# Hybrid retention/HGRN2 step on one core: fewer full warm-up matmuls, row scales of x1 through DRAM, W_v work in the ramp, and a new placement table

## The chip, the cores and the metric

The kernel runs on one core of one Trainium2 chip. The metric is the device time of one launch in microseconds. Each launch is timed as a whole; a profiled launch gives the span from the first to the last instruction and what every engine did in it: PE (TensorE matmul), PEld (TensorE weight load), DVE (VectorE), ACT (ScalarE), POOL (GpSimd) and SP (SyncE, which here only issues DMAs).

## The reference

One layer of a decoder: 2048 prompt tokens and 8 single new tokens, width 1024. The normalised input is projected to eight groups of 512 columns (q, k, v and gate of retention; q, forget, input and gate of HGRN2), two chunked recurrences with 4 heads each run over the tokens, their outputs are normalised and gated, joined, projected, added to the input and normalised again.

```python
h = rmsnorm(x, norm_g)
p = (h @ w_in).astype(jnp.float32)
rq, rk, rv, rg, hq, hf, hi, hgate = jnp.split(p, 8, axis=-1)
...
o_ret, s_ret_new = chunked_decay_recurrence(rq, rk, rv, log_gamma, s_ret)   # rq, rk rotated
o_ret = head_rmsnorm(o_ret, ret_g) * jax.nn.silu(rg)
...
o_hg, s_hg_new = chunked_decay_recurrence(silu(hq), kin, hi, logf, s_hg)
o_hg = head_rmsnorm(o_hg, hg_g) * jax.nn.silu(hgate)
y = x + jnp.concatenate([o_ret, o_hg], axis=-1) @ w_out
return rmsnorm(y, final_norm_g), ...      # and the four new states
```

All data are fp32.

## The kernel before

**Products.** The matrix products run in a form with seven instead of eight block products (sums such as S1, S2, T1, T2 of blocks are made first). Every fp32 operand X is split in two fp32r parts, a high part `Xh` and a low part `Xl`, and a product is three matmuls for each pair of blocks (high·high, low·high, high·low). One block product is 12 matmuls of 128x512. Seven of them make a *unit*. Units u = -6 to -1 compute the values (V) of both recurrences, u = 0 to 23 the gates (G), the q and k of HGRN2 (H) and of retention (R) of one head and one half of the tokens each, u = 24 to 31 the output projection (O). Names such as aG, bG, eH are the PSUM banks that the products of a unit fill; x0… and x1… are the blocks of the first and of the second half of the tokens, wo… those of the output weights; r24S, w24S are a unit's raw and split weight blocks.

**The ramp.** Before unit -6 stands a prologue written out in order: loads of the first token block (`tok_load0`, tile x0r) and of the W_v weights (`wv_load`, tile wvr), their splits (`x_split0`, `wv_split`), and plain products `pv` of the first half row (lines 465 to 650) while the sums and differences of the W_v blocks (`wv_subs`, `wv_parts`: the T1 to T4 and their splits) are made. 13 matmuls of 128x128 and 17 of 32x8 on a tile of ones (`wu`, lines 200 and 203) go ahead of the first product. Each of these fp32 matmuls stands in the profile as two records.

**The queue of events.** Everything that is not a block product is put between the products by `at(pos, f)`: `f` is issued when the products have come to position `pos`, counted in products (7 to a unit, fractions inside a product). The positions stand in one table, `AT`, written by hand; for unit u most are `7 * u + AT[...]`. The engines' queues are in order, so the table sets what stands ahead of what on PE, DVE, ACT, POOL and SP:

```python
SLOTS = (
    (0, "A11", "B11", "A", True), (1, "S1", "T1", "E", True), (3, "S2", "T2", "A", False),
    (4, "S4", "B22", "E", False), (5, "A12", "B21", "B", True), (6, "S3", "T3", "A", False),
    (9, "A22", "T4", "A", False),
)
```

gives the seven products with their place, their weight-side and token-side operand and their bank.

**The parts that the change touches.** `hgrn_rec` and `ret_rec` are the recurrence of one head: scores (`plh`, `pah`, 32x16 and 32x64 matmuls, lines 1223 to 1284, which read the tiles qth and kh that DVE has scaled, lines 1188 and 1191), state updates, outputs and norms; their steps are placed by `AT['hgrn']` and `AT['ret']`. `swap_events` replaces the token blocks x0… by x1… (positions `AT['swap']`, base 77) and then by the output weights wo… (`AT['swapo']`, base 161): a DMA of 1 MB (line 1465), a split on ACT (line 709) and one on DVE (line 713). `blocks_sums` makes the token-block sums of V units with `less` (line 434), whose 16 subtractions of 128x512 stand partly on DVE, partly on POOL. The tokens' row scales `rs_all` hold one token on each partition; to scale x1 blocks along their free axis, `x1_dg` puts them on diagonals (DVE), `x1_spread` multiplies by ones (PE, tile prb, line 701), copies (ACT, line 702) and stores 256 KB to `rb_dram` (POOL, line 1327), which `x1_rb` loads again (line 1345). The same is done in small for the new tokens (`decode_dg`, `decode_spread`, tile prsd). The last half row of the output (`i == 7`) ends with an add to the residual (tile xro, line 716), a square sum (line 1639), a power on POOL (line 1650), the scaling and two stores.

Of the kernel before, what the change touches and what calls it, by code (L numbers as in the profile page):

```python
# [24 lines left out]
NB = 8  # L25
# [23 lines left out]
def spooled(u):  # L49
# [10 lines left out]
          'load': 18.0,  # L60
# [10 lines left out]
 'ret': {'load': 12.0,  # L71
# [4 lines left out]
         'o0': 15.5,  # L76
         'st1': 15.7,
         'o1': 17.1,
         'last': 17.6,
         't0': 19.01,  # L80
         't1': 21.7},
# [6 lines left out]
       'sS1': -1.4,  # L88
# [3 lines left out]
       'sA12': 1.4,  # L92
       'sS3': 2.4,
       'sA22': 3.05},
 're': {'A11': -3.4, 'S1': -2.4, 'S2': -1.4, 'S4': -0.4, 'A12': 0.6, 'S3': 1.6, 'A22': 2.6},
 'dec': {'mm': -1.97, 'mm0': -3.42, 'copy': -0.9, 'copy0': -2.4, 'sel': 0.7},
# [6 lines left out]
          'lT4': 12.2,  # L103
          'B11': (3.0, 3.0, 3.5, 3.5),
          'T1': (6.5, 6.5, 7.0, 7.0),
          'T2': (8.2, 8.2, 8.7, 8.7),
          'B22': (8.9, 8.95, 9.2, 9.75),
          'B21': (9.45, 9.85, 10.0, 10.3),
          'T3': (11.3, 11.3, 11.8, 11.8),
          'T4': (14.2, 14.2, 14.7, 14.7)},  # L110
# [11 lines left out]
           'B21': (9.45, 9.85, 10.0, 10.3),  # L122
           'T3': (11.3, 11.55, 11.8, 12.05),
           'T4': (14.2, 14.2, 14.7, 14.7)},
 'x1': (21.0, 41.0, 48.0, 63.0),
 'x1s': (0.5, 1.8, 1.9, 3.4, 5.0),
 'wo': (27.0, 69.0, 101.8, 122.8),
 'wos': (0.0, 2.3, 3.3),
 'wu': 17,
 'wop': (140.0, 1.8, 2.0, 2.6),  # L130
 'gate': {'G': 0.7, 'store': 1.2, 'R': 0.8, 'H': 0.7, 'root': 0.5, 'scale': 1.0, 'gt': 1.2, 'tr': 0.6},
 'fin': 0.75,
# [11 lines left out]
 'dhs': (-5.0, -2.2, -2.2, -1.5)}  # L144
# [5 lines left out]
def step_kernel(ctx, tc, a, out):  # L150
# [22 lines left out]
    vd_dram = dr.tile([2, NB, GW], F32, tag="vd_dram", name="vd_dram")  # L173
    v_dram = [
# [24 lines left out]
    for n in range(13):  # L199
        pe.matmul(wu, ones, ones, start=True, stop=True)  # L200
# [146 lines left out]

    spread_to = {}

# [74 lines left out]
    def blocks_sums(i, n):  # L424
# [8 lines left out]
        def less(o, x, y):  # L433
            (dve if (i, n) in ((6, 0), (7, 1)) else pool).tensor_tensor(o, x, y, op=ALU.subtract)
# [35 lines left out]
    def tok_load0(i, k0, cuts=1):  # L470
        r = x0r[i, k0] = t_get([P, 2, 256], f"x0r{i}{k0}")
        for n in range(0, 2, 2 // cuts):
            kk = slice(n, n + 2 // cuts)
            sp.dma_start(r[:, kk], a["x_t"][V_ORDER[i], :, k0 + kk.start : k0 + kk.stop])
# [101 lines left out]
    dgd = vq.tile([NB, NB], F32, tag="dgd", name="dgd")  # L576

    def decode_dg():
        dve.tensor_scalar(dgd, ident[:NB, :NB], rsd[:, 1:2], None, op0=ALU.mult)

    def decode_spread():
        pt = ps_tr.tile([P, NB], F32, tag="tr", name="prsd")
        pe.matmul(pt, ones[:NB, :], dgd, start=True, stop=True)
        rb = vq.tile([P, NB], F32, tag="rbd", name="rbd")
        act.activation(rb, pt, AF.Copy)
        dve.tensor_tensor(
            xz[:, : 32 * KT].rearrange("p (k b) -> p k b", b=32)[:, :, :NB], xs,
            rb.unsqueeze(1).to_broadcast([P, KT, NB]), op=ALU.mult,
        )
# [11 lines left out]
    tok_load0(0, 0, 2)  # L601
    wv_load(0, 2)
    act.activation(lb[:, 0:1], zero, AF.Sigmoid)
    tok_load0(0, 4)
    wv_load(4, 2)
    for k in (0, 4):
        x_split0(0, k)
        wv_split(k)
    wv_load(1)
    wv_load(5)  # L610
    for k in (1, 5):
        x_split0(0, k)
        wv_split(k)
    tok_load0(0, 2)
# [12 lines left out]
    sp.dma_start(pk, a["pack"])  # L627
    stats(1)
    decode_inputs()
    for k in range(KT):  # L630
        x_split0(1, k)
    pv0 = {(c, ty): bank([P, GW], f"pv0{c}{ty}") for c in range(2) for ty in range(2)}
# [5 lines left out]
    for m, k in enumerate((0, 4, 1, 5, 2, 6, 3, 7)):  # L638
        decode_values(m, k)
    first, second = ("T1", "T2"), ("T3", "T4")  # L640
# [9 lines left out]
    with tc.manual_schedule(engines=ORDERED):  # L650
        stats_load(2)
        for c in range(2):
            for ty in range(2):
                plain_out(0, c, ty, pv0[c, ty])
        wv_subs(0, first + second)
        wv_parts(0, first + second)
        tok_load(2)
        ps = plain_next(0, 1)
        stats_sum(2, True)
        stats_load(3)  # L660
        wv_subs(1, first + second)
# [1255 lines left out]
```

## Time and profile before

| | |
|---|---|
| time, median of 3 runs | 1006.27 us (1005.38 to 1006.46) |
| the profiled execution's own time | 1006.96 us |
| its span, first to last instruction | 1005.2 us |
| mean granted TensorE clock | 0.998 |
| PE busy | 987.3 us (98%), 8824 matmul records |
| DVE / ACT / POOL busy | 783.6 / 574.6 / 256.2 us |
| DMA moved | 244.56 MB, mean 243 GB/s |

PE is busy in nearly the whole span. The time outside the span is 1006.96 - 1005.2 = 1.8 us. Where PE idles is listed by the view of waits: each row names the instruction that waited, what it waited for, the total, the number of waits and the longest. "issue" in it is a wait for nothing that the profile shows.

### The profile page before, as it was taken

Reading aid. Unit: us, or ns where it says so; the run is one execution under the profiler, and the core shown is the slowest. Engines: PE = TensorE matmul, PEld = TensorE weight load, DVE = VectorE, ACT = ScalarE, POOL = GpSimd, SP = SyncE. Lnnn points to the kernel's source line nnn. Section 1 sums busy time; section 2 is a strip of 40 time slices with the busy share of each in tenths; the row PEclk is TensorE's granted clock in tenths of the full one; section 3 lists DMA queues with packets and bytes.
Section 4 is the critical chain, followed back from the end, with each engine's and each line's share of the span. In section 5 each row is a group of like instructions: output and inputs, shape, how many; then the busy total and the mean of one; then the engine's idle time right before and its main releaser. Section 6 shows DMA issues by size and latency. Waiting matters only on the chain.

```text
span 1005.2 us, 22979 instructions
## 1 busy us (share of the span) xinstructions
PE 987.3 (98%) x8824; PEld 822.0 (82%) x8824; DVE 783.6 (78%) x1361; ACT 574.6 (57%) x1348; POOL 256.2 (25%) x404
## 2 busy tenths in 40 slices
PE   9999999999999999999999999999999999999997
PEld 8788877888888888888788788888888878877885
DVE  6797696879869978887898766877866799767774
ACT  7754523847655664765885555456467577524332
POOL 0211271112332433232012222222222602313121
PEclk9999999999999999999999999999999999999999
DMA  9746659838958878785985993993996396674522
GB/s 332 242 150 238 222 189 357 313 114 298 305 171 306 304 239 287 279 253 184 348 261 175 303 321 119 304 335 109 309 370 218 111 406 228 238 263 155 206 88 83
DMA packets 121340, 244.56 MB, mean 243 GB/s; under 512 B 12128, under 2 KB 52448, under 8 KB 118544
## 3 DMA queue, kind: packets, MB, share of 16 engines
q1 hardware_dynamic: 97968, 164.68, 48.9%
q0 software_dynamic: 22976, 78.17, 21.0%
q8 instruction: 69, 1.13, 0.5%
q14 instruction: 39, 0.32, 0.1%
q10 hardware_dynamic: 288, 0.27, 0.1%
HBM read 155.97 MB, written 90.24 MB: 245 GB/s over the span
## 4 chain that ended last, share of the span: by engine, by line
PE 84%; DVE 7%; ACT 4%; issue 2%; DMA 1%; POOL 1%; POOLq 0%; SPq 0%; DVEq 0%; ACTq 0%
PE aH L872 9%; PE aG L872 8%; PE aO L872 7%; PE aR L872 7%; PE aV L872 5%; PE eG L872 4%; PE eH L872 4%; PE pv L465 4%; PE eO L872 4%; PE eR L872 3%; PE eV L872 2%; PE bH L872 2%; PE bG L872 2%; PE bO L872 2%; PE bR L872 2%
## 5 line engine op out<-in xcount | busy, mean ns | idle before, releaser
L1639 ACT ACTIVATE yj<-xro 128x512 f32<-128x512 f32 x24 | 15.2, 632 | 66.9 <-DVE xro L716 33.2
L1202 ACT ACTIVATE qh<-kh 128x1024 f32<-128x1024 f32 x24 | 25.5, 1061 | 47.3 <-DVE kh L1188 47.3
L1188 DVE TENSOR_TENSOR kh<-kh,fph 128x512 f32<-128x512 f32 x48 | 32.9, 686 | 11.4 <-PE plh L1223 10.5
L949 ACT ACTIVATE sg<-g 128x512 f32<-128x512 f32 x26 | 16.4, 631 | 36.3 <-DVE g L716 35.8
L1082 ACT ACTIVATE obh<-poh 128x128 f32<-128x128 f32 x64 | 16.9, 287 | 32.5 <-PE poh L1078 32.5
L1191 DVE TENSOR_TENSOR qth<-qth,fph 128x512 f32<-128x512 f32 x48 | 32.9, 685 | 0.0
L1082 ACT ACTIVATE obr<-por 128x128 f32<-128x128 f32 x64 | 16.8, 276 | 27.3 <-PE por L1078 27.3
L716 DVE TENSOR_TENSOR xro<-aO,xro 128x512 f32<-128x512 f32 x33 | 22.5, 685 | 8.1 <-PE aO L872 7.8
L1106 POOL DMA_DIRECT2D o_dram<-gth x16 | 12.4, 773 | 62.6 <-DVE gth L1103 23.4
L1090 ACT ACTIVATE obh<-poh,orsh 128x128 f32<-128x128 f32 x64 | 18.2, 366 | 16.5 <-POOL orsh L229 16.4
L336 POOL TENSOR_TENSOR ms<-ms 128x2 f32<-128x2 f32 x8 | 3.0, 370 | 95.4 <-ACT xn L332 95.4
L956 POOL DMA_DIRECT2D g_dram<-g x31 | 16.9, 548 | 39.0 <-DVE g L952 33.9
L1090 ACT ACTIVATE obr<-por,orsr 128x128 f32<-128x128 f32 x64 | 18.2, 368 | 14.6 <-POOL orsr L229 14.6
L228 POOL TENSOR_SCALAR orsh<-omsh 128x4 f32<-128x4 f32 x16 | 4.9, 308 | 84.1 <-ACT obh L1082 83.8
L902 ACT ACTIVATE vo<-aV 128x512 f32<-128x512 f32 x12 | 7.1, 592 | 32.4 <-PE aV L872 32.1
L1069 DVE SCALAR_TENSOR_TENSOR sth<-sth,fph,puh 128x128 f32<-128x128 f32 x48 | 16.7, 347 | 11.0 <-PE poh L1078 8.5
L1106 POOL DMA_DIRECT2D o_dram<-gtr x16 | 12.5, 782 | 46.3 <-DVE g L716 14.0
L1076 PE MATMUL poh<-vh,A 128*128 128x128 f32 x128 | 24.0, 274 | 0.0
L1076 PE MATMUL por<-vr,A 128*128 128x128 f32 x128 | 24.0, 274 | 0.0
L228 POOL TENSOR_SCALAR orsr<-omsr,pk 128x4 f32<-128x4 f32 x16 | 7.6, 474 | 57.5 <-ACT obr L1082 57.5
L1653 DVE SCALAR_TENSOR_TENSOR xro<-xro,yms,fg 128x1024 f32<-128x1024 f32 (+1 forms) x16 | 19.9, 1245 | 3.0 <-POOL yms L1650 3.0
L1078 PE MATMUL poh<-sth,qth 128*128 128x128 f32 x112 | 21.7, 275 | 0.0
(1712 smaller groups left out, 3760.0 us busy)
## 6 DMA issues: line engine op xcount, KB each, us to landing
xn<-in_x_prompt SPq DMA_DIRECT2D x32, 256.0 KB, 4.7
v_dram<-vo SPq DMA_DIRECT2D x32, 256.0 KB, 3.4
xro<-in_x_prompt SPq DMA_DIRECT2D x16, 512.0 KB, 5.8
g_dram<-g POOLq DMA_DIRECT2D x31, 256.0 KB, 5.6
out_y_prompt<-xro POOLq DMA_DIRECT2D x15, 512.0 KB, 3.4
xr<-in_x_t SPq DMA_DIRECT2D x12, 512.0 KB, 5.7
vh<-v_dram SPq DMA_DIRECT2D x16, 256.0 KB, 8.0
gth<-g_dram SPq DMA_DIRECT2D x16, 256.0 KB, 6.8
```

Source lines behind the costliest of these rows:

```text
L465: pe.matmul(ps, xx, ww, start=(first and n == 0), stop=(last and n == 2))
L716: dve.tensor_tensor(o, x, y, op=ALU.add)
L872: pe.matmul(ps, w[i], x[j], start=(first and k == 0 and m == 0), stop=(k == 3 and m == 2), skip_group_check=True,)
L1076: pe.matmul(po[:, j], s_ctx["A"][:, c], box["v"][g][:, j], start=True, stop=src is None)
L1078: pe.matmul(po[:, j], qcol(c), src, start=False, stop=True)
L1082: act.activation(ob[:, j], po[:, j], AF.Square, accum_out=ms[:, j : j + 1])
L1090: act.activation(ob[:, j], po[:, j], AF.Copy, scale=rs[:, j : j + 1])
L1106: after(AT["gate"]["tr"], lambda: pool.dma_start(o_dram[c0 : c0 + 4, ty, :, h].rearrange("c p t -> p c t"), gt.rearrange("p (c t) -> p c t ...
L1188: dve.tensor_tensor(kv[:, :, 0, :], kv[:, :, 0, :], two[:, :, 1:2].to_broadcast([P, nb, b]), op=ALU.mult)
L1191: dve.tensor_tensor(qv[:, :, 1, :], qv[:, :, 1, :], two[:, :, 0:1].to_broadcast([P, nb, b]), op=ALU.mult)
L1202: act.activation(kept_k, k, AF.Copy)
L1653: dve.scalar_tensor_tensor(x[:, cc], x[:, cc], ms[:, 0:1], fg[:, cc], op0=ALU.mult, op1=ALU.mult)
```

## The change

It has seven parts: the warm-up has 9 full and 27 tiny matmuls; the first loads are cut into halves; part of the W_v work and of the new tokens' work moves forward in the ramp, into the first products; the row scales of x1 (and of the new tokens) go to DRAM as they are and are loaded as broadcast rows; all subtractions of `blocks_sums` are on DVE; many places in the table move; and the last half row of the output is added and squared in two halves of 256 columns.

```diff
@@ the table AT: a few of its rows
- 'ret': {'load': 12.0, ... 'o0': 15.5, ... 'last': 17.6, 't0': 19.01, 't1': 21.7},
+ 'ret': {'load': 12.5, ... 'o0': 15.0, ... 'last': 17.1, 't0': 19.51, 't1': 23.2},
@@ swap
-          'lT4': 12.2,
+          'lT4': 12.7,
-          'T4': (14.2, 14.2, 14.7, 14.7)},
+          'T4': (14.05, 14.05, 14.7, 14.7)},
@@ swapo
-           'lB21': 6.4,
+           'lB21': 6.9,
...
+ 'hd': ((0.0, 0.0, 0.0, 0.0), (0.0, 0.0, -0.5, -0.5), (0.0, 0.0, 0.0, 0.0), (0.3, 0.0, 0.0, 0.0),
+        (0.0, 0.0, 0.0, 0.0), (0.0, 0.5, 0.0, 0.0), (0.0, 0.0, 0.0, 0.0), (0.0, 0.0, 0.0, 0.5)),
+ 'retL': {...}, 'hgrnL': {...}, 'w24': (-6.1, -2.4, -1.9, -0.95, -0.45),
@@ where the table is used
-        for n, pos in AT["ret" if u % 3 else "hgrn"].items():
+        kind = "ret" if u % 3 else "hgrn"
+        for n, pos in AT[kind + "L" if u > 20 else kind].items():
+            if n in ("s0", "s1", "s2", "s3"):
+                pos += AT["hd"][u // 3][int(n[1])]
             at(7 * u + pos, lambda n=n: do(n))
@@ warm-up
-    for n in range(13):
+    for n in range(9):
         pe.matmul(wu, ones, ones, start=True, stop=True)
     for n in range(AT["wu"]):          # 17 before, 27 now
@@ first loads
-    tok_load0(0, 0, 2)
+    tok_load0(0, 0, (0,))
     wv_load(0, 2)
     act.activation(lb[:, 0:1], zero, AF.Sigmoid)
-    tok_load0(0, 4)
+    tok_load0(0, 4, (0,))
     wv_load(4, 2)
+    tok_load0(0, 0, (1,))
+    tok_load0(0, 4, (1,))
@@ between the first products
+        if kk == 1:
+            decode_inputs()
+            for m, k in enumerate((0, 4, 1, 5)):
+                decode_values(m, k)
+            for k in range(2):
+                wv_subs(k, first + second)
+                wv_parts(k, first + second)
@@ row scales
+    def rows_store(c):
+        pool.dma_start(rs_dram[c : c + 4].rearrange("c p -> p c"), rs_all[:, c : c + 4])
...
-        sp.dma_start(xd["rb"], rb_dram[n])
+        c = 8 + 4 * TB[n]
+        sp.dma_start(xd["rb"].rearrange("p (c t) -> p c t", c=4), rs_dram[c : c + 4].partition_broadcast(P))
...
-    for n in range(2):
-        at(9.2 + n, lambda n=n: x1_dg(n))
-        at(10.6 + n, lambda n=n: x1_spread(n))
...
+    for n in range(2):
+        at(-24.2 + 4 * n, lambda n=n: rows_store(8 + 4 * n))
@@ blocks_sums
         def less(o, x, y):
-            (dve if (i, n) in ((6, 0), (7, 1)) else pool).tensor_tensor(o, x, y, op=ALU.subtract)
+            dve.tensor_tensor(o, x, y, op=ALU.subtract)
@@ the last half row
+        elif i == 7:
+            for m in range(2):
+                cc = slice(256 * m, 256 * m + 256)
+                add(xb[:, cc], ps[:, cc], xb[:, cc])
+                y_sq(cb, 2 * m, cc)
+            y_out(cb, True)
@@ y_out
         pool.tensor_tensor(ms[:, 0:1], ms[:, 0:1], ms[:, 1:2], op=ALU.add)
+        if last:
+            pool.tensor_tensor(ms[:, 0:1], ms[:, 0:1], ms[:, 2:3], op=ALU.add)
```

The order of the instructions shows three of the places. On PE, at the end of unit 21's H recurrence: `plh` are the last score matmuls, `aR` a block product of unit 23. Before:

```order
2777 L872 MATMUL bR_9731<-x1B21h,w23A_9493 128x512
2778 L1275 MATMUL plh_9757<-fh_8871,qh_8905 32x32 x16
2779 L1284 MATMUL plh_9758<-qth_9177,kh_9066 32x64 x16
2780 L872 MATMUL aR_9454<-x1T3h,w23S_9592 128x512
2781 L872 MATMUL aR_9454<-x1T3l,w23S_9592 128x512
2782 L872 MATMUL aR_9454<-x1T3h,w23S_9592 128x512 x2
```

The same place now:

```order
2795 L914 MATMUL bR_9720<-x1B21h,w23A_9561 128x512
2796 L914 MATMUL aR_9431<-x1T3h,w23S_9487 128x512
2797 L914 MATMUL aR_9431<-x1T3l,w23S_9487 128x512
2798 L914 MATMUL aR_9431<-x1T3h,w23S_9487 128x512 x2
2799 L914 MATMUL aR_9431<-x1T3l,w23S_9487 128x512
2800 L914 MATMUL aR_9431<-x1T3h,w23S_9487 128x512
2801 L1317 MATMUL plh_9752<-fh_8852,qh_8889 32x32 x16
2802 L1326 MATMUL plh_9753<-qth_9186,kh_9056 32x64 x16
```

The first six matmuls of the block product now stand ahead of the scores.

On SP, where the output weights' blocks are loaded into the places of x1 blocks that are no longer read (woB21, woB22; xro are rows of the prompt). Before:

```order
405 L1463 DMA woT2h<-preT2h 128x2048
406 L1463 DMA woT2l<-preT2l 128x2048
407 L1465 DMA woB21l<-t_dram 128x2048
408 L1632 DMA xro_9823<-in_x_prompt 128x1024
409 L1632 DMA xro_9826<-in_x_prompt 128x1024
410 L1465 DMA woB22l<-t_dram 128x2048
411 L1624 DMA fg<-in_final_norm_g 128x1024
```

Now:

```order
410 L1486 DMA woT2h<-preT2h 128x2048
411 L1486 DMA woT2l<-preT2l 128x2048
412 L1655 DMA xro_9797<-in_x_prompt 128x1024
413 L1655 DMA xro_9800<-in_x_prompt 128x1024
414 L1488 DMA woB22l<-t_dram 128x2048
415 L1488 DMA woB21l<-t_dram 128x2048
416 L1647 DMA fg<-in_final_norm_g 128x1024
```

The load of woB21 went from ahead of the two xro loads to behind woB22.

On DVE, in the last V units, where `bs…` and `bT…` are the token-block sums, `vo` adds a V product to its row and x0B11l is a split. Before:

```order
160 L394 TENSOR_TENSOR S1S_1487<-S1S_1487,xr_1271 128x512
161 L716 TENSOR_TENSOR vo_1479<-eV_1412,vo_1479 128x512
162 L233 TENSOR_TENSOR x0B11l<-xr_1271,x0B11h 128x4x256
163 L272 TENSOR_TENSOR s7S_1512<-S1S_1487,s7S_1512 128x512
164 L716 TENSOR_TENSOR vo_1408<-bV_1505,vo_1408 128x512
165 L434 TENSOR_TENSOR bT_1527<-bs71B_1468,xr_1271 128x512
```

Now:

```order
165 L433 TENSOR_TENSOR S1S_1496<-S1S_1496,xr_1285 128x512
166 L270 TENSOR_TENSOR x0B11l<-xr_1285,x0B11h 128x4x256
167 L756 TENSOR_TENSOR vo_1488<-eV_1421,vo_1488 128x512
168 L473 TENSOR_TENSOR bT_1508<-bs70B_1455,xr_1285 128x512
169 L473 TENSOR_TENSOR bT_1509<-bs70B_1457,bT_1508 128x512
170 L473 TENSOR_TENSOR bs70B_1455<-bs70B_1457,bs70B_1455 128x512
171 L473 TENSOR_TENSOR bs70B_1457<-xr_1286,bT_1509 128x512
172 L309 TENSOR_TENSOR s7S_1521<-S1S_1496,s7S_1521 128x512
173 L756 TENSOR_TENSOR vo_1417<-bV_1514,vo_1417 128x512
```

Four subtractions that POOL had done stand between the two adds to vo, and the split of x0B11 stands ahead of the first of them.

More of the change, by code (lines that the diff above doesn't have):

```diff
@@ L59 @@
           's2': 17.6,
-          'load': 18.0,
+          'load': 17.5,
           's3': 19.7,
@@ L70 @@
           't1': 28.2},
- 'ret': {'load': 12.0,
+ 'ret': {'load': 12.5,
          's': 11.55,
@@ L697, in step_kernel @@
     dve.tensor_copy(lmask, packed("lmask"))
-    def blk_spread(blk, dg, dst):
-        pt = ps_tr.tile([P, 4, P], F32, tag="tr", name=f"prb{blk}")
-        for j in range(4):
-            pe.matmul(pt[:, j], ones, dg[:, j], start=True, stop=True)
-        act.activation(dst, pt.rearrange("p a b -> p (a b)"), AF.Copy)
     def raw(b):
```

204 lines of the change are left out of this document (109 added, 95 removed).

## The prediction

> **What bounds the kernel now.** I read the page first: the busy shares, the chain that ended last, the DMA queues.
>
> ```profile
> PE 987.3 (98%) x8824; PEld 822.0 (82%) x8824; DVE 783.6 (78%) x1361; ACT 574.6 (57%) x1348; POOL 256.2 (25%) x404
> PE 84%; DVE 7%; ACT 4%; issue 2%; DMA 1%; POOL 1%; POOLq 0%; SPq 0%; DVEq 0%; ACTq 0%
> q8 instruction: 69, 1.13, 0.5%
> ```
>
> PE is busy 987.3 of 1005.2 us, and 84% of the chain is PE. The time can fall in three ways only: less work on PE, fewer waits of PE, or shorter ends, before the first product and behind the last. So the next view is who PE waited for (total, times, longest).
>
> ```profile
> PE plh L1284 <- DVE qth L1191: 2.2, 2, 1.5
> PE plh L1223 <- issue: 2.0, 2, 1.0
> PE pah L1223 <- issue: 1.5, 1, 1.5
> ...
> PE aO L872 <- DVE xro L716: 0.9, 1, 0.9
> PE par L1140 <- DVE qr L716: 0.7, 1, 0.7
> PE poth L1101 <- DVE gth L1103: 0.6, 1, 0.6
> PE plh L1223 <- DVE qth L1191: 0.5, 2, 0.3
> PE aV L872 <- DVE vo L716: 0.4, 1, 0.4
> PE eH L872 <- DVE x1T1l L713: 0.4, 1, 0.4
> ```
>
> Waits on DVE sum to 2.2 + 0.9 + 0.7 + 0.6 + 0.5 + 0.4 + 0.4 = 5.7 us; waits for nothing that the profile shows ("issue") to 3.5 us. Those 9.2 us are all that placing can win, and every one of the first kind is DVE being late by less than 1.5 us.
>
> **Warm-up and first loads.** The timeline of the first microseconds, with the tile view's row of the full warm-up matmuls (min, median, max ns):
>
> ```profile
> 1.12 4.86 PE L200 MATMUL wu<-ones 128*128 128x128 f32 x26 [1.12 <-POOL ones L191]
> 5.92 0.48 PE L203 MATMUL wu<-ones 128*32 128x8 f32 x34
> L200 PE MATMUL wu<-ones x26: 275/421/579, 1.1 to 5.7; 128*128 128x128 f32 x26
> 6.33 0.49 PE L465 MATMUL pv<-wvT1h,x0B11h 128*128 128x512 f32 x1
> 6.80 0.50 PE L465 MATMUL pv<-wvT1l,x0B11h 128*128 128x512 f32 x1
> 5.39 0.63 ACT L232 ACTIVATE wvT1h<-wvr 128x512 fp32r<-128x512 f32 x1 [1.02 <-DMA wvr<-in_w_v]
> 6.05 0.69 DVE L233 TENSOR_TENSOR wvT1l<-wvr,wvT1h 128x512 fp32r<-128x512 f32 x1 [1.17 <-ACT wvT1h L232]
> ```
>
> 26 records take 4.8 us, from 1.12 to 5.92, or 0.185 each on average; eight fewer end 1.5 us earlier at that mean. The 34 tiny records take 5.92 to 6.33, or 0.012 each; 20 more cost 0.24 us. So PE is free at 6.33 - 1.5 + 0.24 = 5.1. The first product also needs wvT1h, done at 5.39 + 0.63 = 6.02, and the second wvT1l, done at 6.74, 0.06 us before its start at 6.80: after the warm-up it is the load of W_v that sets the start. That load now stands behind one 128 KB DMA instead of two, which is worth about one issue on SP, some 0.4 us, and a little less traffic ahead. I take -0.6 us for the ramp; the ends are 0 (the load lands no earlier) and -1.2 (6.33 - 5.1, PE's bound). The W_v and new-token work that moves into the first products is DVE, ACT and POOL work under 48 us of PE products. It is hidden as long as DVE holds its order there. The extra loads are four DMAs on SP ahead of nothing that the first products need.
>
> The Trainium skill ("TensorE: Matmul & The Clock Gate", Part 1) speaks against a shorter warm-up: it says that the clock rises after some 3.4 us of activity in a window that runs freely, so that the moment varies from run to run. The trace has one such rise, and the late case is among the rivals below.
>
> **Row scales of x1.** The spread on PE, twice 8 records, and the small one for the new tokens:
>
> ```profile
> 205.69 1.05 PE L701 MATMUL prb<-dgx,ones 128*128 128x128 f32 x8
> 206.50 0.47 PE L872 MATMUL eG<-x0B22h,w1S 128*128 128x512 f32 x1
> 206.82 0.39 PE L872 MATMUL eG<-x0B22l,w1S 128*128 128x512 f32 x1
> 207.04 0.63 PE L872 MATMUL eG<-x0B22h,w1S 128*128 128x512 f32 x2
> ...
> 127.30 0.39 PE L872 MATMUL bV<-wvT4h,x0B21l 128*128 128x512 f32 x1
> 127.62 0.38 PE L583 MATMUL prsd<-dgd,ones 8*128 8x8 f32 x2
> 127.93 0.50 PE L872 MATMUL aV<-T3h,s5S 128*128 128x512 f32 x1
> ```
>
> A matmul of 128x512 follows the next in 0.22 us (206.82 to 207.04), but in 0.32 behind the spread. So one spread costs 206.50 - 205.69 = 0.81 and 0.10 behind it, 0.9 us; two cost 1.8. prsd costs 127.93 - 127.30 - 0.22 = 0.4. PE has nothing else to do there, so this is on the path: -2.2 us. What is added are three small POOL stores and a changed load of the same size; the loads come long after the stores (over 40 products for x1, some seven for the new tokens), and POOL is 25% busy. Nothing is added for them; a late one would be seen as a wait of DVE. Two DVE operations, two ACT copies and two stores of 256 KB go as well, off the path.
>
> **The subtractions of block sums.** DVE's busy time in the V units, one POOL subtraction, POOL's idle time for a load ahead of them, and a DVE addition without and with POOL at work beside it:
>
> ```profile
> 125.00:150.00 25.00, 25.00 (x111) 20.03 (x110) 23.18 (x31) 7.38 (x13) 19.39 (x19) 1.00 0.55 182
> L434 POOL TENSOR_TENSOR bs70B<-bs70B,bs70B x1: 1745/1745/1745, 145.3 to 145.3; 128x512 f32<-128x512 f32 x1
> DMA bs70B<-x_dram: 1.4, 1
> L394 DVE TENSOR_TENSOR S<-S,xr x5: 691/693/693, 50.4 to 123.9; 128x512 f32<-128x512 f32 x5
> L394 DVE TENSOR_TENSOR S1S<-S1S,xr x1: 1666/1666/1666, 146.0 to 146.0; 128x512 f32<-128x512 f32 x1
> ```
>
> The same addition takes 0.69 us five times and 1.67 us at 146.0, where POOL subtracts: DVE loses about a microsecond to one POOL subtraction of 1.7. DVE is busy 23.18 of 25 us there. The eight subtractions cost DVE 8 x 0.69 = 5.5 us; if each of them on POOL held DVE up by 0.5 to 1.0 us, their going gives 4 to 8 back. I take DVE as no worse off, and the wait of 0.4 at 151 (aV on vo) as gone: -0.4. The ends are -0.4 and the loss worked out as the second rival.
>
> **Moved places.** The largest single wait and its cause, and the load behind the wait of `par`:
>
> ```profile
> 814.80 0.65 PE L1284 MATMUL plh<-qth,kh 128*32 128x64 f32 x32 [1.49 <-DVE qth L1191]
> 813.97 0.69 DVE L1191 TENSOR_TENSOR qth<-qth,fph 128x512 f32<-128x512 f32 x1
> ...
> 818.77 0.90 SPq L1465 DMA_DIRECT2D woB22l<-t_dram  x1
> 828.40 2.00 ACT L709 ACTIVATE woB22h<-woB22l 128x1024 fp32r<-128x1024 f32 x2 [4.50 <-DMA woB22l<-t_dram]
> ```
>
> In unit 21 PE stood still 1.49 us for qth, which ended at 814.66. Six matmuls of the next product (6 x 0.22 = 1.3 us) now stand ahead: -1.3. Near 840 PE waited 0.7 for `par`: ACT had stood 4.5 us for woB22l, which SP had issued behind woB21l and two xro loads, and DVE then had the splits of both blocks to do together. With woB22 ahead of woB21 that pile comes apart: -0.7 there, and of the 0.6 at poth ten microseconds later, in the same pile, half: -0.3. The two short waits of plh L1223 on qth (0.5 together) had a weight split ahead of qth on DVE; it is moved: -0.4, since other loads' work now stands near. The waits of aO (0.9), eH (0.4) and the other 0.7 of plh L1284 have the same DVE work ahead of them as before: 0. Together -2.7 us; the ends are 0 (every wait finds a new cause) and -4.7 (all gone).
>
> What the moved places can newly make late is unknown. The nearest rows are the waits just listed, 0.4 to 1.5 us each, in eight places of the run. I add one such wait of middle size, +0.7; the ends are 0 and +3. The likeliest place is x1T4: its load is issued half a product later and its split on ACT stands a little earlier, while
>
> ```profile
> DMA to landing us min/median/max: 7.4/10.0/12.1
> ```
>
> is how long such 1 MB loads take. ACT would then stand for it with bank evictions queued behind.
>
> **Issue gaps.** One of the three:
>
> ```profile
> 297.24 0.26 PE L1223 MATMUL pah<-qth,kh 128*32 128x16 f32 x8 [1.54 <-issue]
> ```
>
> All three lie inside bursts of 64 small matmuls, not ahead of them. The instruction queue q8 brought 69 packets, 17648 records of PE and PEld make 256 for each, and counted along PE's instructions the three gaps stand 194, 195 and 194 above a multiple of 256. I read them as PE running ahead of its instruction fetch where a burst of short instructions meets a packet's start. The change takes out and adds a few dozen instructions, so the starts fall elsewhere: none to six of some 69 may hit, and I take three again: 0, with ends -3.5 and +3.5.
>
> The Trainium skill ("Runtime: NRT & Kernel Launch", Instruction fetch mechanics) gives blocks of 256 instructions and says that crossing one is mostly hidden; the size agrees with 17648 / 69, while three gaps of 1.0 to 1.5 us would not be hidden. By its rule this term and its ends would be 0, and the sum the same.
>
> **The tail.** The last half row:
>
> ```profile
> 997.96 0.69 DVE L716 TENSOR_TENSOR xro<-aO,xro 128x512 f32<-128x512 f32 x1 [0.49 <-PE aO L872]
> 998.68 0.63 ACT L1639 ACTIVATE yj<-xro 128x512 f32<-128x512 f32 x1 [1.00 <-DVE xro L716]
> 999.56 0.19 POOL L1649 TENSOR_TENSOR yms<-yms 128x1 f32<-128x1 f32 x1 [0.57 <-ACT yj L1639]
> ```
>
> Add, then square, then POOL. In halves the second add lies beside the first square, but a second reading of the accumulator and a POOL addition of 0.19 come in; the first of the two additions needs only the first half and hides. I take -0.2; ends -0.5 and +0.3.
>
> **The sum.** -0.6 - 2.2 - 0.4 - 2.7 + 0.7 + 0 - 0.2 = -5.4 us. Against the profiled execution, 1006.96, that is 1001.6; its own time stands 0.7 above the median of the runs, 1006.27, and from the median it is 1000.9. I forecast 1000.9 us, with 998.5 to 1003 as this case's own range.
>
> **Rivals.** What a measurement can tell from no change is 0.2%, 2 us: below 1004.3 is faster, above 1008.3 slower.
>
> *The waits only move.* Every wait on DVE that goes comes back where DVE is late next, since its work is the same and its share 78%. Then PE's removed work, the ramp and the tail are left: -2.2 - 0.6 - 0.2 = -3.0, or 1003.3. For it speaks that DVE is the releaser of all of them; against it that the wait of 1.5 and the pile at 840 have a cause of their own place. Chance 0.22.
>
> *DVE falls behind in the V units: slower.* If the subtractions on POOL are not why DVE's operations there were long, DVE gets 5.5 us more on 23.18 of 25, and with them POOL's wait for a load (1.4 us, bs70B), which then holds up vo behind it; with two such waits that is 5.5 + 2.8 - 1.8 (25 - 23.18) = 6.5 us of delay. vo frees the bank that the next V product writes, so PE stands as long: -5.4 + 6.5 = +1.1, 1007.4. It decides from 5.4 us of delay on. Against it: the addition that took 1.67 us beside POOL and 0.69 otherwise. Chance 0.07, a part of it beyond 1008.3.
>
> *Gaps of the fetch multiply, or the clock rises late.* Three or four more gaps at 1.0 to 1.5 us would give 1000.9 + 3.5 = 1004.4. A late clock: the warm-up's records took 421 ns in the middle and 275 at the shortest, late ones; if the first dozen matmuls of 0.22 us ran slower by that ratio, 1.5, that is 12 x 0.22 x 0.5 = +1.3, or 1002.2, inside the forecast's own range. Chance 0.11 together.
>
> **How the numbers follow.** Forecast 0.60, waits move 0.22, fetch or clock 0.11, DVE behind 0.07. Below 998.5 lies a part of the first case (fetch gaps gone), which I leave at 0.06 below 998.0. Above 1004.5 lies most of DVE behind, half of fetch or clock, and a little of the waits that move beyond their price, 0.14 together. So the range is 998.0 to 1004.5. Faster by more than 0.2%: 0.60 + 0.19 + 0.05 = 0.84; within: 0.11; slower: 0.05.
>
> **What the profile after would show.** First pv near 5.7 instead of 6.33. No prb and no prsd. DVE additions of 0.69 us through 125 to 150 and no wait of aV on vo. PE's list of waits without the 1.5 of plh L1284 and the 0.7 of par, with DVE's remaining ones summing to about 3.5 us. Issue gaps at other places, still inside bursts of L1265. I am wrong if the list of waits holds new entries of more than 2 us together, if vo is late, or if PE's busy time does not fall by about 3 us.

## The result, and the profile after

| | before | changed |
|---|---|---|
| time, median | 1006.37 us (1005.38 to 1006.86, 4 runs) | 1020.20 us (1019.33 to 1021.32, 4 runs) |
| profiled execution | 1006.96, span 1005.2 | 1021.32, span 1019.5 |
| mean granted TensorE clock | 0.998 | 0.992 |

The ratio is 1.0135, 95% interval 1.012 to 1.015: slower by 13.8 us, where 1000.9, and at most 1004.5, had been forecast. The page of the changed kernel, its busy shares:

```profile
PE 988.1 (97%) x8818; PEld 820.3 (80%) x8818; DVE 782.2 (77%) x1367; ACT 576.0 (56%) x1347; POOL 247.9 (24%) x398
```

PE's busy time did not fall, although the spreads are gone, and the span grew by 14.3 us. Half clock hides the fall: PE ran at 0.5 from 151.3 to 154.2 us and from 417.0 to 420.4, which costs about 1.4 + 1.7 = 3.1 us of busy time (an estimate: half of each stretch), and 988.1 - 3.1 = 985.0 is 2.3 below before. The view of waits of PE names most of the growth:

```profile
PE prs L402 <- DVE dg L395: 11.3, 2, 10.5
PE plh L1265 <- issue: 3.7, 2, 2.2
PE aV L914 <- DVE xz L626: 2.4, 1, 2.4
PE aV L914 <- ACT vo L634: 1.8, 1, 1.8
PE pkh L1081 <- DVE kh L1230: 1.1, 1, 1.1
...
PE plh L1326 <- issue: 0.6, 1, 0.6
```

Of the old waits, those at 815 (1.5), 840, 850, 919 and 489 are not in the list any more. What is new is one wait of 10.5 us and some of 1 to 2.4. I took from both traces when the first product of each stage starts and subtracted:

| from, to | changed minus before, us | what the trace shows there |
|---|---|---|
| start to first V product | +2.1 | first product 1.1 earlier, then waits of 0.8 (prs) and 1.8 (vo) |
| first V product to unit 0 | +13.3 | waits of 2.4 and 10.5, then PE at half clock |
| unit 1 to 2 | -1.8 | the spread of the x1 scales is gone |
| unit 8 to 9 | +3.7 | an issue gap of 2.2 instead of 1.0, then half clock |
| unit 9 to 23 | -2.0 | short waits and a gap of before gone |
| unit 23 to 28 | -1.5 | waits of before gone, a gap of 1.5 and a wait of 1.1 new |
| rest of the span | +0.5 | units 0 to 1, 2 to 8, 28 to the end |

So the question is the stretch from 107 to 155 us. On the timeline (start, duration, idle time before and its releaser), DVE's last two operations before the hole, the one behind it, the diagonal that PE waits for, and PE:

```profile
134.30 0.68 DVE L756 TENSOR_TENSOR vo<-bV,vo 128x512 f32<-128x512 f32 x1
134.90 0.22 DVE L626 TENSOR_TENSOR xz<-pk,rbd 128x64 f32<-128x64 f32 x1
145.81 0.69 DVE L473 TENSOR_TENSOR bT<-bs61B,xr 128x512 f32<-128x512 f32 x1 [10.70 <-DMA v_dram<-vo]
150.88 0.48 DVE L395 TENSOR_SCALAR dg<-ident,rs_all 128x128 f32<-128x128 f32 x2
151.31 1.19 PE L402 MATMUL prs<-dg,ones 128*128 128x128 f32 x4 [10.47 <-DVE dg L395]
```

DVE stood 10.7 us until a V row's store had landed: the tile that the sum bT goes to is one of the temporaries that such a store frees. The view of DMAs from 124 to 150 us has these stores at a median of 12.2 us to landing (first list); in the same stretch before it was 2.0 (second list; 3.4 over the whole run).

```profile
v_dram<-vo SPq DMA_DIRECT2D x3, 256.0 KB, 12.2
...
rs_dram<-rs_all POOLq DMA_DIRECT2D x1, 2.0 KB, 12.2
```

```profile
v_dram<-vo SPq DMA_DIRECT2D x5, 256.0 KB, 2.0
```

In the list of the changed kernel stands what the change added: a store of row scales, 2 KB, that took 12.2 us to land. It is 512 pieces of 4 bytes, because it writes along the partitions. The line view of its first issue (107.0) and second (132.5):

```profile
L386 POOL DMA_DIRECT2D rs_dram<-rs_all x1: 855/855/855, 107.0 to 107.0; - x1
DMA to landing us min/median/max: 10.8/10.8/10.8
...
L386 POOL DMA_DIRECT2D rs_dram<-rs_all x1: 778/778/778, 132.5 to 132.5; - x1
DMA to landing us min/median/max: 12.2/12.2/12.2
```

The windows around them (columns: the stretch and its length, busy us of PE, PEld, DVE, ACT and POOL with counts, granted clock, DMA's busy share, GB/s):

```profile
110.00:118.00 8.00, 8.00 (x37) 6.61 (x36) 4.00 (x8) 1.54 (x2) 0.00 (x0) 1.00 0.87 38
118.00:132.00 14.00, 14.00 (x65) 11.66 (x64) 9.27 (x17) 7.39 (x16) 1.43 (x2) 1.00 0.80 242
132.00:138.00 6.00, 3.57 (x17) 2.65 (x16) 3.08 (x6) 0.00 (x0) 3.31 (x5) 1.00 0.88 173
138.00:145.00 7.00, 2.83 (x13) 2.02 (x11) 0.00 (x0) 0.00 (x0) 0.00 (x0) 0.92 1.01 104
145.00:151.00 6.00, 0.00 (x0) 0.00 (x0) 5.12 (x9) 2.99 (x5) 4.36 (x6) 0.50 0.73 255
151.00:155.00 4.00, 3.69 (x12) 3.17 (x13) 4.00 (x9) 0.07 (x1) 0.73 (x1) 0.60 0.95 279
```

While the first store is under way the engines are 87% busy and move 38 GB/s, against 242 in the next row. PE does not feel that one in these 8 us (8.00 of 8.00), but it does later. In e5_late, the experiment that differs by the place of the two stores alone, SP has issued the loads of a token row by 114.4 us; here the last goes out at 118.9, of which 1.8 are the later start of the V units. ACT then waits for these rows, DVE for ACT and PE for DVE. The first of these lines is e5_late's, the others are the changed kernel's:

```profile
112.56 1.82 SPq L361 DMA_DIRECT2D xn<-in_x_prompt  x4
...
114.35 4.98 SPq L361 DMA_DIRECT2D xn<-in_x_prompt  x4
126.51 0.63 ACT L369 ACTIVATE xn<-xn 128x512 f32<-128x512 f32 x1 [2.19 <-DMA xn<-in_x_prompt]
129.31 1.22 DVE L270 TENSOR_TENSOR x0B11l<-xr,x0B11h 128x1024 fp32r<-128x1024 f32 x1 [3.48 <-ACT x0B11h L269]
135.13 0.47 PE L914 MATMUL aV<-wvT1h,x0B11h 128*128 128x512 f32 x1 [2.43 <-DVE xz L626]
```

That is the wait of 2.4, and it is over before the second store's packets begin (136.2). e5_late has no such wait; what holds SP up row by row is not shown. The second store stops DVE, ACT and POOL for 7 us. And PE, idle for 10 us, is granted half clock from 144 on: behind the wait five matmuls take 2.2 us (152.15 to 154.31) instead of 1.1.

### The profile page after: what moved, and what is told of

It is laid out like the page before. It is cut to its first block, busy times and chain, and to the rows that moved or that the text cites. A ratio compares the mean times of both kernels' runs of the same rounds, so it can differ in the third digit from the quotient of the medians.

```text
span 1019.5 us, 22943 instructions
## 1 busy us (share of the span) xinstructions
PE 988.1 (97%) x8818; PEld 820.3 (80%) x8818; DVE 782.2 (77%) x1367; ACT 576.0 (56%) x1347; POOL 247.9 (24%) x398
## 5 line engine op out<-in xcount | busy, mean ns | idle before, releaser
L1663 ACT ACTIVATE yj<-xro 128x512 f32<-128x512 f32 (+1 forms) x28 | 17.3, 616 | 73.1 <-DVE xro L756 40.4
L1230 DVE TENSOR_TENSOR kh<-kh,fph 128x512 f32<-128x512 f32 x48 | 33.0, 687 | 15.4 <-PE plh L1265 12.9
L1681 DVE SCALAR_TENSOR_TENSOR xro<-xro,yms,fg 128x1024 f32<-128x1024 f32 (+1 forms) x16 | 20.0, 1248 | 13.8 <-POOL yms L1678 13.8
L756 DVE TENSOR_TENSOR xro<-aO,xro 128x512 f32<-128x512 f32 (+1 forms) x34 | 22.6, 668 | 5.9 <-PE aO L914 5.9
L373 POOL TENSOR_TENSOR ms<-ms 128x2 f32<-128x2 f32 x8 | 5.3, 667 | 81.1 <-ACT xn L369 81.1
L369 ACT ACTIVATE xn<-xn 128x512 f32<-128x512 f32 x32 | 19.9, 624 | 7.1 <-DMA xn<-in_x_prompt 7.1
L1120 PE MATMUL por<-str,qr 128*128 128x128 f32 x112 | 21.7, 275 | 0.0
L1118 PEld LDWEIGHTS por<-vr,A 128*128 128x128 f32 x128 | 20.3, 191 | 1.3
L1118 PEld LDWEIGHTS poh<-vh,A 128*128 128x128 f32 x128 | 20.3, 191 | 1.2
```

The source lines that it names most:

```text
L369: act.activation(r, r, AF.Square, accum_out=ms[:, 2 * h + j : 2 * h + j + 1])
L756: dve.tensor_tensor(o, x, y, op=ALU.add)
L1118: pe.matmul(po[:, j], s_ctx["A"][:, c], box["v"][g][:, j], start=True, stop=src is None)
L1120: pe.matmul(po[:, j], qcol(c), src, start=False, stop=True)
L1230: dve.tensor_tensor(kv[:, :, 0, :], kv[:, :, 0, :], two[:, :, 1:2].to_broadcast([P, nb, b]), op=ALU.mult)
L1663: act.activation(jk[:, : cc.stop - cc.start], xro[c][:, cc], AF.Square, scale=D ** -0.5, accum_out=yms[c][:, n : n + 1])
```

## The experiments

Three theories stood against each other: the row stores jam the DMA engines (and DVE's new subtractions suffer from it); the eight subtractions overload DVE, the second rival of the prediction; the ramp is late. Times are medians, ratios are against the kernel before on the same chip (its medians 1006.1 to 1006.3).

**e1_x1pe: the spread on PE again.**

```diff
+    def x1_dg(n): ...            # as before the change
+    def x1_spread(n): ...
-        at(-24.2 + 4 * n, lambda n=n: rows_store(8 + 4 * n))
+        at(9.2 + n, lambda n=n: x1_dg(n))
+        at(10.6 + n, lambda n=n: x1_spread(n))
```

> The changed kernel with the x1 row scales spread on PE again (diagonals, 8 matmuls, 256 KB stores); everything else as changed. Theory 'jam': the two stores of rs_all in 4-byte pieces fill the DMA engines for some 10 us each (110 to 118 and 133 to 145 us), so DVE's subtractions wait for their loads and PE for DVE. Without them the waits of prs on dg (10.5) and of aV on xz (2.4) go and the spread costs 1.8 again: 1020.2 - 12.9 - 1.4 (half clock behind the wait) + 1.8 = about 1007.7, DVE idle before bs61B under 2 us. Rival 'DVE overload': the eight subtractions on DVE are the cause by themselves: the waits stay and the time is about 1022.

1004.06 us, ratio 0.999 (0.9974 to 1.0005). The waits of 10.5 and 2.4 are gone, the clock is 0.998. The time lies 3.6 us below my sum and 2.3 below the kernel before; the interval still holds 1, so this alone does not show that the rest of the change gains anything.

**e4_tp: the rows turned on PE and stored as 4 rows of 512 bytes.**

```diff
-        pool.dma_start(rs_dram[c : c + 4].rearrange("c p -> p c"), rs_all[:, c : c + 4])
+        pt = ps_tr.tile([P, P], F32, tag="tr", name=f"prt{c}")
+        pe.matmul(pt[:4], rs_all[:, c : c + 4], ident, start=True, stop=True)
+        rt = vq.tile([4, P], F32, tag="rst", name=f"rst{c}")
+        act.activation(rt, pt[:4], AF.Copy)
+        after(0.5, lambda: pool.dma_start(rs_dram[c : c + 4], rt))
...
-        at(-24.2 + 4 * n, lambda n=n: rows_store(8 + 4 * n))
+        at(-23.4 + 7 * n, lambda n=n: rows_store(8 + 4 * n))
```

> The changed kernel with the rows turned by one matmul against the identity and stored as 4 rows of 512 bytes instead of 512 pieces of 4 bytes. Theory 'jam': landing about 2 us, no wait of prs on dg over 2 us, 1020.2 - 12.9 - 1.4 + 0.5 = about 1006.4. Rival 'DVE overload': no change, 1020.

1004.88 us, ratio 0.9988 (0.9971 to 1.0005), with no wait of prs on dg. The stores also stand 0.8 and 3.8 products later in the table, but the first is issued at the same time as in the changed kernel (107.3 against 107.0). The same 2 KB now land in 2.0 us, and the stretch behind the first store moves 252 GB/s instead of 38:

```profile
L390 POOL DMA_DIRECT2D rs_dram<-rst x1: 602/602/602, 107.3 to 107.3; - x1
DMA to landing us min/median/max: 2.0/2.0/2.0
...
110.00:118.00 8.00, 8.00 (x39) 6.67 (x38) 4.48 (x8) 1.70 (x3) 0.72 (x1) 1.00 0.72 252
```

Same bytes, same destination, almost the same time, other pieces: the jam comes from the store's 4-byte pieces and not from its bytes.

**e2_lesspool: the subtractions on POOL again, row stores as changed.**

```diff
-            dve.tensor_tensor(o, x, y, op=ALU.subtract)
+            (dve if (i, n) in ((6, 0), (7, 1)) else pool).tensor_tensor(o, x, y, op=ALU.subtract)
```

> The changed kernel with the eight subtractions of block sums on POOL again; row stores as changed. Theory 'jam': the DMA engines are jammed just as long, but POOL and not DVE waits for the loads, so the wait of prs on dg shrinks from 10.5 to under 3 us: about 1009 to 1012. Rival 'jam alone is enough' (ACT and SP stand for the same jam): 1018 to 1021. Rival 'DVE overload': 1007 to 1009 and no jam to be seen.

1018.90 us, ratio 1.0128 (1.0099 to 1.0158). My theory had said that DVE would then pass the jam by. It did not. DVE's next operation, another sum, needed a temporary all the same:

```profile
145.39 0.69 DVE L437 TENSOR_TENSOR S<-xr 128x512 f32<-128x512 f32 x1 [12.03 <-DMA v_dram<-vo]
```

**e3_brows: the kernel before with the row stores alone.**

> The kernel before with the row stores alone (x1 row scales through DRAM as in the change, no spread on PE); subtractions on POOL, table and ramp as before. Theory 'jam': 512 pieces take some 10 us of DMA each time, but nothing on PE's path waits: 1006.3 - 1.8 = 1004.5, at most 1008 if the V units' loads come late. Rival 'jam alone is enough': 1012 or more, with a wait of PE near 140 us. Rival 'no jam': landing under 5 us and 1004.5.

1021.35 us, ratio 1.0154 (1.0139 to 1.0169). The edit removes 1.8 us of PE work and costs 15. Again DVE and then PE:

```profile
145.55 0.69 DVE L402 TENSOR_TENSOR S<-xr 128x512 f32<-128x512 f32 x1 [12.97 <-DMA v_dram<-vo]
150.96 0.76 PE L367 MATMUL prs<-dg,ones 128*128 128x128 f32 x2 [12.67 <-DVE dg L360]
```

So the jam alone is enough, and the interaction with the subtractions that I had proposed falls.

**e7_bless: the kernel before with the eight subtractions on DVE alone.**

> The kernel before with the eight subtractions of block sums on DVE and nothing else. Forecast of the prediction: DVE's operations beside POOL's shrink to 0.69 us, the wait of aV on vo (0.4) goes: 1005.9. Rival 'DVE falls behind': 1007.4 or more, with a wait of PE between 125 and 160 us.

1006.92 us, ratio 1.0007 (0.9994 to 1.0021): no change to be measured. DVE did get faster, as I had said: from 125 to 150 us it did 39 operations in 22.32 us, where the kernel before did 31 in 23.18, and the addition that had taken 1.67 us took 0.69.

```profile
125.00:150.00 25.00, 25.00 (x113) 20.25 (x112) 22.32 (x39) 7.90 (x14) 8.04 (x12) 1.00 0.55 184
```

But the wait of aV on vo stayed (0.49 at 151.75, 0.39 before). DVE's overload falls as well.

**e5_late: the changed kernel with the row stores 29 and 32 products later.**

```diff
-        at(-24.2 + 4 * n, lambda n=n: rows_store(8 + 4 * n))
+        at(5.0 + 7 * n, lambda n=n: rows_store(8 + 4 * n))
```

> The changed kernel with the two row stores (512 pieces of 4 bytes each, as changed) issued 29 and 32 products later, in units 0 and 1, where no V row is waiting for its store. Theory 'ring': the store holds the DMA engines some 10 us wherever it is, but it costs PE time only where temporaries wait for stores to land; here it costs under 2 us: 1004 to 1007, landing again 9 to 13 us. Rival 'ten us anywhere': 1012 or more.

1003.23 us, ratio 0.9971 (0.9954 to 0.9988): the fastest of all, faster than both kernels. The stores take as long as ever,

```profile
L386 POOL DMA_DIRECT2D rs_dram<-rs_all x1: 765/765/765, 188.0 to 188.0; - x1
...
DMA to landing us min/median/max: 11.4/11.4/11.4
```

and from 188 to 200 us PE is busy 12.00 of 12.00. The transfer is as slow; here nothing that PE waits for needs a landing in those 11 us. That is the whole 17 us between this kernel and the changed one.

**e6_dose: the kernel before with four more stores, of 128, 256, 512 and 896 pieces of 4 bytes, that nothing reads.**

> The kernel before with four further stores of row scales to a tile that nothing reads, one unit apart in units 8 to 11: 1, 2, 4 and 7 columns, that is 128, 256, 512 and 896 pieces of 4 bytes. Theory: the landing time grows with the number of pieces, some 20 ns a piece: about 4, 6, 12, 20 us. Rival 'bytes decide': all land in 2 to 4 us. Rival 'one-time jam in the V units only': 512 pieces land in under 5 us here.

Its one run took 1007.01 us, inside the range of the kernel before (1003.83 to 1009.69): stores that nothing reads cost nothing that one run could show. The trace has landings for two, the 256 pieces and the 896:

```profile
L350 POOL DMA_DIRECT2D ds_dram<-rs_all x1: 789/789/789, 431.5 to 431.5; - x1
...
DMA to landing us min/median/max: 10.0/10.0/10.0
...
L350 POOL DMA_DIRECT2D ds_dram<-rs_all x1: 992/992/992, 489.3 to 489.3; - x1
...
DMA to landing us min/median/max: 12.9/12.9/12.9
```

Time did not grow with the pieces as I had said: 256 take 10.0, 512 took 8.2 to 13.5 in the other kernels, 896 take 12.9. What sets the 10 us stays open.

**e8_act: turned rows, and in the ramp the squares of the third token row behind the evictions on ACT again.**

```diff
         stats_load(2)
-        stats_sum(2, True)
...
         ps = plain_next(0, 1)
+        stats_sum(2, True)
         spread_dg(2)
```

> The changed kernel with the turned rows (4 rows of 512 bytes), and in the ramp the squares of the third token row (stats_sum(2)) behind the four evictions of the first row on ACT again, as before the change. Theory 'ACT order': the V rows are stored earlier, SP reaches the fourth row's loads some 5 us earlier, and the wait of aV on vo (L634, 0.5 to 1.8 us) and that of prs on dg go: 0.5 to 1.5 us below the kernel with turned rows (1004.9): 1003.4 to 1004.4. Rival 'no matter': within 0.3 us of 1004.9.

1005.30 us, ratio 0.9998 (0.9985 to 1.0011). The wait of aV on vo is gone, and the V units start at 55.28 instead of 55.65 in e4_tp: 0.4 us, no more than the starts differ between kernels of the same ramp (55.06 in e11_tiny41, 55.25 in e5_late). The time is not lower than e4_tp's; its trace has an issue gap of 2.2 us at 403 with 3.4 us of half clock behind it, where e4_tp has a gap of 1.4 and no half clock.

**e9_ramp: e5_late with the ramp of before** (13 full and 17 tiny warm-up matmuls, the old order of loads and of the W_v work).

> The changed kernel with the late row stores and the ramp as before the change (13 full and 17 tiny warm-up matmuls, the old order of loads, W_v work and new tokens' work). Forecast of the prediction: the new ramp is worth 0.6 us, so 1003.8. Theory 'the ramp gives nothing': the first product starts 0.2 to 1.1 us earlier, and aV on vo (ACT) takes it back: 1002.7 to 1003.4, V units starting within 0.3 us of each other.

1007.63 us, ratio 1.0004 (0.9989 to 1.0018). The V units start at 55.19, in e5_late at 55.25: the new ramp gives nothing. The 4.4 us on top are elsewhere: the issue gaps of its trace sum to 7.6 us against 3.8 in e5_late, and one of them, at 812, takes 4.7. The next pair says what these gaps are.

**e10_tiny18 and e11_tiny41: e5_late with 18 and with 41 tiny warm-up matmuls.**

```diff
- 'wu': 27,
+ 'wu': 18,        # e10_tiny18; 41 in e11_tiny41
```

> The changed kernel with the late row stores and 18 instead of 27 tiny warm-up matmuls: 36 instructions fewer at the head of PE's stream and nothing else (each tiny matmul is 4). Theory 'fetch': gaps named issue fall where a block of 256 instructions begins; every start now lies 36 instructions later in the work, so the gap of 2.1 us at 399 us shrinks or goes with the half clock behind it, and the one at 807 goes; any gap lies again 194 to 197 above a multiple of 256 of the new stream. Time 1001 to 1002.5. Rival 'gaps belong to the bursts': the same gaps of 2.1 and 1.2 us at 399 and 807, 1003.2.

> The changed kernel with the late row stores and 41 instead of 27 tiny warm-up matmuls: 56 instructions more at the head of PE's stream. Theory 'fetch': the starts of blocks lie 56 instructions earlier in the work; gaps move to about 313 and 461 us, where a block holds nearly only short matmuls, none at 399 and 807; a gap over 2 us is followed by 3.4 us at half clock. Time 1003 to 1007. Rival 'gaps belong to the bursts': the same gaps at 399 and 807.

1011.68 us (ratio 1.0044, 1.0018 to 1.007) and 1016.42 us (1.0087, 1.0066 to 1.0109). A handful of 12 ns matmuls on a tile of ones moved the median by 8 and 13 us against e5_late. The gaps of PE's timeline, first e10_tiny18, then e11_tiny41:

```profile
401.45 0.40 PE L1265 MATMUL plh<-qth,kh 128*32 128x16 f32 x12 [2.29 <-issue]
566.38 0.36 PE L1265 MATMUL plh<-qth,kh 128*32 128x16 f32 x19 [1.16 <-issue]
813.07 0.50 PE L914 MATMUL eR<-x1B22h,w23S 128*128 128x512 f32 x1 [2.62 <-issue]
```

```profile
318.00 0.59 PE L914 MATMUL aR<-x0T2h,w5S 128*128 128x512 f32 x1 [4.88 <-issue]
469.82 0.18 PE L1265 MATMUL pah<-qth,kh 128*32 128x16 f32 x1 [2.70 <-issue]
718.04 0.79 PE L914 MATMUL aG<-x1T3h,w19S 128*128 128x512 f32 x1 [2.67 <-issue]
```

I counted each gap's place in PE's own stream of instructions (weight loads, matmuls, waits, in order of their start):

| run | gap at, us | place in the stream | above a multiple of 256 |
|---|---|---|---|
| before | 297, 400, 557 | 4290, 6851, 10178 | 194, 195, 194 |
| changed | 254, 312, 416, 825 | 3267, 4291, 6850, 15811 | 195, 195, 194, 195 |
| e5_late | 296, 399, 807 | 4291, 6850, 15811 | 195, 194, 195 |
| e10_tiny18 | 401, 566, 813 | 6850, 10434, 15811 | 194, 194, 195 |
| e11_tiny41 | 318, 470, 562, 718 | 5058, 8130, 10179, 13507 | 194, 194, 195, 195 |
| e9_ramp | 231, 238, 402, 812 | 3010, 3266, 6851, 15810 | 194, 194, 195, 194 |

All 48 such gaps of the fourteen traces (of 0.2 us and more) lie 194 or 195 above a multiple of 256. The work that stands there moved with the shift, as theory 'fetch' says; the places at 313 and 461 that I had named for e11_tiny41 were hit within 10 us. That PE waits for its instructions there can be read in the packets of the instruction queue, 16 KB each: every one of the 48 gaps ends 1.2 to 1.8 us after such a packet has landed. 47 of these packets took 0.9 to 1.8 us (the other 3.8), so it is their start that is late.

The other half of the theory missed: in e10_tiny18 the gaps at 399 and 807 did not shrink or go, they grew to 2.3 and 2.6. My times were far off, too: I had expected 1001 to 1002.5 and 1003 to 1007, since I did not foresee that a gap can reach 4.9 us, nor what follows it. The spans of the profiled executions are 1001.4 (e5_late), 1007.0 and 1012.2. Of the 5.6 us that e10_tiny18 takes longer, longer gaps are 2.2, more half clock, behind them and behind a wait of 1.8 in the ramp, some 3.4, other waits 0.3; of the 10.8 of e11_tiny41 the gaps are 6.8, half clock some 1.9, other waits 1.6. The medians lie 2.9 and 2.5 above the profiled executions, and the ten runs of e10_tiny18 go from 1004.0 to 1018.1; that part no trace shows. In the windows of the changed kernel around its gap at 414 to 416:

```profile
414.00:416.40 2.40, 0.23 (x26) 0.13 (x15) 0.00 (x0) 0.00 (x0) 1.29 (x2) 1.00 1.00 381
416.50:420.00 3.50, 3.50 (x38) 2.80 (x38) 1.81 (x4) 2.26 (x4) 0.55 (x1) 0.57 0.95 356
```

Behind 2.2 us of idleness PE ran some 3.4 us at half clock, which costs up to 1.7 us more. The DMA engines were fully busy during the gap (1.00).

**e12_out: the kernel before with two of the moved places alone** (woB21's load behind woB22's, unit 21's last scores half a product later).

```diff
-            'lB21': 6.4,
+            'lB21': 6.9,
...
-            'B21': (9.45, 9.85, 10.0, 10.3),
+            'B21': (9.45, 9.85, 10.25, 10.55),
...
+            if u == 21 and n == "s3":
+                pos += 0.5
```

> The kernel before with two of the moved places alone: the load of woB21 behind that of woB22 (6.9 instead of 6.4, its splits later), and the last scores of unit 21 half a product later. Forecast of the prediction: waits of 1.3 at 815, 0.7 at 840 and 0.3 at 850 go: 1006.1 - 2.3 = 1003.8. Rival 'waits only move': within 0.8 us of 1006.1, with new waits of PE between 815 and 920.

1008.50 us, ratio 1.0011 (0.9996 to 1.0026): no gain. The three waits did shrink or go (1.5 to 0.45 at 817, none near 840 and 850), and this came in their place:

```profile
822.18 1.04 PE L1039 MATMUL pkh<-ident,kh 128*128 128x128 f32 x7 [3.29 <-DVE kh L1188]
```

The scores end later, and DVE now scales kh at 821.35, behind three operations on kr and sw (lines 967, 968 and 716) that stood behind it before, when it was scaled at 817.58; the state update waits for it. 3.4 us of half clock follow that wait. In the whole change, where the steps of the last units are placed anew as well, a wait of 1.1 (changed) or 0.7 (e5_late) on kh is left.

## Why the prediction was wrong

- **Row scales, the step that failed.** "Nothing is added for them; a late one would be seen as a wait of DVE." It was seen so: 10.7 us of DVE, 10.5 + 2.4 of PE and 1.4 at half clock. I priced the stores by their 2 KB and looked for their readers, which come 40 products later. But the price is not in the bytes (as 4 rows of 512 bytes the same 2 KB landed in 2.0 us), and it is paid by the other transfers of those 11 us: the V rows' stores, and with them the temporaries that DVE waits for. The nearest row, a store of 256 KB in whole rows that landed in 2.4 us, was no bound for it, and I had set no upper end.
- **The gain of that step was right:** units 1 to 2 are 1.8 us shorter with the spread gone (e4_tp, e5_late: 1.8 each), as worked out. From the first V product to unit 0, e5_late gains 1.45; 0.4 was forecast for prsd and 0.4 for the wait of aV on vo. Both are gone there. What removed the wait is open, since the subtractions alone leave it (e7_bless), and so is the rest of the gain.
- **The ramp: 0.6 forecast, nothing found.** The first product starts earlier: 5.2 to 6.1 us in the eight traces with the new ramp, 6.3 to 7.4 in the six with the old, 0.9 on average against 0.6 forecast. But the V units start at 55.1 to 57.0 against 54.9 to 56.0, and e9_ramp has them where e5_late has. "It is hidden as long as DVE holds its order there" was the wrong engine in the changed kernel: on ACT the squares of the third token row now stand ahead of the evictions; they wait for their load, the splits of that row's sums wait for what hangs on the squares, and the last eviction comes behind these splits:

```profile
47.46 0.63 ACT L369 ACTIVATE xn<-xn 128x512 f32<-128x512 f32 x1 [2.54 <-DMA xn<-in_x_prompt]
55.02 1.36 ACT L308 ACTIVATE s2S<-S 128x512 fp32r<-128x512 f32 x2 [3.73 <-DVE S L432]
56.28 0.67 ACT L634 ACTIVATE vo<-pv,rs_all 128x512 f32<-128x512 f32 x1
57.01 0.50 PE L914 MATMUL aV<-wvT1h,x0B11h 128*128 128x512 f32 x1 [1.77 <-ACT vo L634]
```

  With the squares put back (e8_act) that wait is gone, but e5_late has the same order on ACT and a wait of 0.36; what makes it 1.8 in two executions (changed, e10_tiny18) is not shown.

- **Subtractions: -0.4 forecast, nothing found** (e7_bless), although DVE gained what I had read from the rows. The rival, DVE falling behind by itself, is excluded too. It had the right place and the right next victim, but not the cause.
- **Moved places: -2.7 forecast, and +0.7 for a new wait.** Units 23 to 28 are 2.2 shorter in e5_late, against 2.3 forecast for 815, 840 and 850. The three waits are gone (1.5, 0.7, 0.6), and so is the one at 919 (0.9), which I had put at 0; a wait on kh of 0.7 is new, and an issue gap of 1.2 fell into these units. e12_out shows that the two edits I named don't bring this by themselves: taken alone they give a wait of 3.3 back. That the sum came out near is in part luck: other moves than those that I argued from had their share.
- **Issue gaps: the mechanism was right, the size was not.** I took three gaps again, 0, with an end of +3.5. In the changed kernel they sum to 4.6 us against 3.6 before, and one is followed by half clock; between e5_late and e11_tiny41, 56 instructions cost 13 us in the median. The Trainium skill ("Runtime: NRT & Kernel Launch", Instruction fetch mechanics) has the block of 256 right, which the table of places shows; "mostly hidden" does not hold here, with gaps up to 4.9 us.
- **Clock.** A late rise in the warm-up did not come in the changed kernel: the clock is full from 3.98 us on, the first product starts at 5.24. In four other traces with the new ramp it rose 0.3 to 1.0 us behind the first product. The clock was lost later. The Trainium skill ("TensorE: Matmul & The Clock Gate", Why this matters for your kernels) gives idle gaps of some 3 us as what brings half clock; here a gap of 2.07 us was enough (e5_late), and so was a wait of 1.80 in e10_tiny18, while gaps of 2.10 (e9_ramp) and 2.70 us (e11_tiny41) and a wait of 2.43 (the changed kernel) left the clock at 1.00. The traces show what decides. In each of them the changes of the granted clock lie whole multiples of 3.41 us apart. Cut at these instants, the fourteen traces give 4056 pieces at full clock (without those ahead of the first rise and in the last 6 us); in 15 of them PE idled 1.80 us or more, and each of the 15 was followed by half clock; in the others it idled 1.77 us at most, and none was. So only the part of a gap counts that falls into one piece. Two pieces of e10_tiny18 and two of e11_tiny41 (length, PE busy, clock): the wait of 1.80 lies in one, the gap of 2.70 is cut in 1.52 and 1.18.

```profile
53.33:56.74 3.41, 1.61 (x8) 1.00 0.71 222
56.74:60.15 3.41, 3.41 (x10) 0.50 0.24 85
...
465.22:468.64 3.42, 1.90 (x159) 1.00 0.61 177
468.64:472.05 3.41, 2.23 (x12) 1.00 0.01 2
```

  Where the cuts lie differs between executions (the first rise comes at 3.98 to 7.16 us), so a gap of some 2 us costs half clock in one and not in another.
- **The tail** gained 0.1 (start of the last matmul to the end 7.62 before, 7.53 after; 0.2 forecast).

Without the jam the change is worth 1.5 to 2.9 us (e4_tp, e1_x1pe, e5_late; only e5_late's interval excludes no gain), not 5.4: the ramp's 0.6 is not there, and in e5_late the fetch gaps and the half clock behind one of them take some 2 us more than before (0.3 + 1.7).

## What to carry to other kernels

Price a DMA by how it is cut up and by who else uses the engines while it runs, not by its bytes and its reader: look for what must land in the next 10 us, and either turn the data first or put the store where nothing lands on the path. In a kernel of many short matmuls the place of each block of 256 instructions is a hidden variable of several microseconds; a comparison of two versions that differ in instruction count is only as good as their gaps, so read those first.

## What was not expected of the hardware

A store of 2 KB in 4-byte pieces takes 8.2 to 13.5 us to land in every place where it was tried; 256 and 896 such pieces took 10.0 and 12.9. 256 KB V rows beside it go from 2.0 to 12.2 us; as four rows of 512 bytes the same 2 KB land in 2.0. The clock is decided in pieces of 3.41 us: in these traces 1.80 us of idle PE or more in one of them always brought half clock for the next, 1.77 or less never did, and the stretches at half clock are 3.4 us or a multiple of it. Gaps of up to 4.9 us stand where PE's stream reaches a new block of 256 instructions, and end 1.2 to 1.8 us after that block's packet has landed. What makes the packet start late is not shown: in the changed kernel the DMA engines were full during the gap at 414, but I have no run that changes only that.
